# Weight units loaded seven ahead, up rows in dying buffers, and a new order of splits and fetches in a decoder block

## The chip, the cores and the metric

The kernel runs on one core of a Trainium2 chip. The metric is device time in microseconds for one execution; the median of three runs is given, and beside it the profile of one execution.

The engines are called PE (TensorE, matrix products), DVE (VectorE), ACT (ScalarE), POOL (GpSimd) and SP (SyncE). A core has 16 DMA engines. Plain transfers are issued here by SP and ACT, indirect ones (gathers by a table of row numbers) by GpSimd.

## The reference

One decoder block for 256 tokens of width 2048 in float32: attention and retention in parallel, an output projection, and then a retrieval layer over 16,384 experts, which is the part that the change touches:

```python
def peer(x, w_query, sub_keys, expert_down, expert_up):
    qry = (xt @ w_query).reshape(T, H, 2, PEER_HALF_DIM)
    s = jnp.einsum('thpd,phnd->thpn', qry, sub_keys)
    top_s, top_i = lax.top_k(s, K)                      # K = 16, H = 8
...
    best_s, best_pos = lax.top_k(cand_s.reshape(T, H, K * K), K)
    expert_idx = jnp.take_along_axis(cand_i.reshape(T, H, K * K), best_pos, axis=-1)
    gates = jax.nn.softmax(best_s, axis=-1)
...
        u = expert_down[ib]
        act = jax.nn.gelu(jnp.einsum('td,thkd->thk', xb, u), approximate=False)
        vv = expert_up[ib]
        return jnp.einsum('thk,thkd->td', gb * act, vv)
```

So each token picks 8 × 16 = 128 experts, takes the dot product of its row with each expert's down row, and sums the 128 up rows with the weights gate × gelu(dot product). The block's input is added, and a last RMSNorm follows.

## The kernel before

**Tokens and rows.** The 256 tokens are two blocks of 128, one token on each partition. "Row" below means one gather: for one of the 2 × 128 pairs of block and choice, each partition receives the expert row that its token chose. There are so 256 down rows, 256 up rows (128x2048, 1 MB each) and 256 scores (128x1).

**Up to 888 us** the projections, attention, retention, the output projection and the query projection run, all as matrix products whose float32 weights are cut in two on the way: ACT casts a half of a weight unit (128 x 4 x 512, 1 MB) to the reduced float32 type that PE takes fast (`whi`, line 109) and DVE subtracts that from the original (`wlo`, line 110). Each product of a chunk is then three matmuls: hi·hi, hi·lo, lo·hi. Units are loaded by SP into three buffers `raw`, and `next_unit` (line 126) has a unit loaded and split two ahead of its use.

**The gemm stage, to 1412 us.** The dot products of all tokens with all 16,384 down rows would be 256 x 16,384 numbers over 2048 columns. The kernel computes 11 of the 16 column chunks in this way, on PE, in 32 tiles of 512 experts: 8 chunks as split products (48 matmuls, two units) and 3 chunks unsplit in float32 (12 instructions, one unit, line 163). The result `a`, scaled by ACT (line 479), is written to `a_dram`. The last tile takes all 11 chunks unsplit (line 174). For the other 5 chunks (640 columns) only the chosen experts are wanted. When the indices `ix` of the top-k are ready (line 606), GpSimd gathers the 640 columns of each down row into a ring of eight buffers `v` (`fetch_u`, line 617), and DVE takes 256 dot products (`dot`, line 625), each with its sum in `sdot`. Each dot product issues the fetch eight later, and the last eight issue the first eight up rows in the same buffers (line 595).

**The last stage.** GpSimd fetches the score of each pair of token and expert from `a_dram` into `wsel` (line 652). For each group of eight choices DVE adds the dot products' part (line 694), ACT takes the gelu (line 695), DVE multiplies by the gates (line 696), and then DVE adds the eight up rows, each times its weight, to `ys` in PSUM (line 704). After row n the score n+14 and the up row n+8 are issued (lines 707 to 710), in one fixed line on GpSimd (`in_line`, line 658). `finish` does the last norm and writes the block's output.

**What sets the order.** Each engine runs its own instructions in order and waits by semaphores. Where the code sets no order, a scheduler that works on estimates places the instructions; DVE's background work of the gemm stage (top-k, then dot products) is drawn from a list by costs (`drain`).

## Time and profile before

| what | before |
|---|---|
| median of 3 runs | 2150.22 us (2147.36 to 2151.7) |
| profiled execution | 2149.12 us |
| its span | 2147.3 us |
| busy PE / DVE / ACT / POOL | 1391.4 / 1550.4 / 613.7 / 920.1 us |
| mean granted clock of PE, share of full speed | 0.828 |
| moved by DMA | 630.24 MB, 293 GB/s over the span |

The span is measured from the first to the last instruction on the device, and the profiled execution's time is 1.8 us more. All rows below come from that execution. Times are in us from the span's start, unless marked otherwise; "mean ns" is one instruction's mean duration, and a busy PE is not PE at its peak. In a row of a timeline, the first number is the start, the second how long the run of equal instructions took, `x6` how many they are, and the square brackets give the engine's idle time just before and what ended it ("issue": nothing that the profile shows).

### The profile page before, as it was taken

To read this page: it belongs to the slowest core of one execution; us is meant where nothing else is said; L and a number is where in the kernel's file an instruction comes from. 1 tells how busy PE (TensorE), PEld (TensorE's weight loads), DVE (VectorE), ACT (ScalarE), POOL (GpSimd) and SP (SyncE) were. 2 spreads that over 40 slices of the span, in tenths; PEclk is the share of its full clock that TensorE was granted. 3 is DMA by queue.
4 is the path that set the end of the run, shared out by engine and by line. 5 is a ranking of instruction groups with operands and counts; after the bars stand their busy time and mean duration, and the time that the engine had idled before them with its cause. 6 is when DMAs were issued, how large, how long until landed. Compare 5 with 4: busy or idle time off the path is not lost.

```text
span 2147.3 us, 18694 instructions
## 1 busy us (share of the span) xinstructions
PE 1391.4 (65%) x5848; PEld 1075.2 (50%) x5848; DVE 1550.4 (72%) x2026; ACT 613.7 (29%) x780; POOL 920.1 (43%) x805
## 2 busy tenths in 40 slices
PE   8999999999999999999999999930000000000000
PEld 6888888888888888766666666610000000000000
DVE  5676575545445567896778777739889888988888
ACT  6555444444444454433333333200000001000001
POOL 0101001000000010008888888847667677777774
PEclk9999999999999999999999999965555555555555
DMA  8544445655555564469999999959999999999997
GB/s 301 182 155 173 176 150 185 234 192 190 188 195 196 177 237 170 160 219 369 404 409 408 405 410 401 406 218 399 365 362 399 351 396 356 397 371 370 380 368 316
DMA packets 115604, 630.24 MB, mean 293 GB/s; under 512 B 22448, under 2 KB 23088, under 8 KB 55088
## 3 DMA queue, kind: packets, MB, share of 16 engines
q0 software_dynamic: 65536, 352.50, 42.1%
q1 hardware_dynamic: 38592, 253.77, 32.3%
q10 hardware_dynamic: 11376, 22.77, 2.8%
q8 instruction: 46, 0.75, 0.1%
q14 instruction: 54, 0.44, 0.1%
HBM read 610.10 MB, written 18.87 MB: 293 GB/s over the span
## 4 chain that ended last, share of the span: by engine, by line
PE 45%; issue 16%; DMA 15%; POOL 11%; DVE 8%; POOLq 4%; ACT 0%; ACTq 0%; DVEq 0%; SPq 0%
PE acc L141 13%; PE acc L142 13%; PE acc L140 12%; DMA v<-in_down_g_dram,ix 10%; POOL v L595 4%; POOL wsel L652 4%; DVE ys L704 4%; POOLq L595 3%; DMA v<-in_up_dram,ix 3%; POOL v L617 2%; DVE wlo L110 2%; POOLq L652 1%; PE acc L163 1%; DVE djunk L625 1%; DMA wsel<-a_dram,ix 1%
## 5 line engine op out<-in xcount | busy, mean ns | idle before, releaser
L110 DVE TENSOR_TENSOR wlo<-raw,whi 128x1024 fp32r<-128x1024 f32 (+1 forms) x422 | 522.0, 1239 | 331.7 <-ACT whi L109 330.7
L704 DVE SCALAR_TENSOR_TENSOR ys<-v,wsel,ys 128x2048 f32<-128x2048 f32 x252 | 593.5, 2355 | 63.3 <-DMA v<-in_up_dram,ix 41.9
L109 ACT CAST whi<-raw 128x1024 fp32r<-128x1024 f32 (+1 forms) x422 | 439.6, 1048 | 664.8 <-PE acc L142 369.6
L617 POOL DMA_INDIRECT v<-in_down_g_dram,ix x256 | 342.3, 1337 | 258.3 <-issue 226.0
L595 POOL DMA_INDIRECT v<-in_up_dram,ix x256 | 259.6, 1014 | 114.3 <-issue 94.4
L652 POOL DMA_INDIRECT wsel<-a_dram,ix x256 | 259.6, 1014 | 100.6 <-issue 77.7
L141 PE MATMUL acc<-wlo,xth 128*128 128x512 f32 x736 | 292.9, 398 | 0.5 <-DVE wlo L110 0.5
L142 PE MATMUL acc<-whi,xtl 128*128 128x512 f32 x736 | 288.9, 393 | 0.0
L625 DVE SCALAR_TENSOR_TENSOR djunk<-v,rs_r,hg 128x640 bf16<-128x640 f32 x256 | 218.9, 880 | 96.5 <-DMA v<-in_down_g_dram,ix 89.8
L140 PE MATMUL acc<-whi,xth 128*128 128x512 f32 x736 | 267.4, 395 | 8.9 <-ACT whi L109 8.9
L157 PE MATMUL acc<-wlo,hth 128*128 128x512 f32 x496 | 196.8, 397 | 9.5 <-DVE wlo L110 5.7
L158 PE MATMUL acc<-whi,htl 128*128 128x512 f32 x496 | 193.7, 391 | 0.0
L156 PE MATMUL acc<-whi,hth 128*128 128x512 f32 x496 | 186.0, 412 | 1.7 <-ACT whi L109 1.7
L695 ACT ACTIVATE wsel<-wsel 128x8 f32<-128x8 f32 x32 | 6.7, 208 | 626.8 <-DVE wsel L694 215.1
L163 PE MATMUL acc<-raw,htf 128*128 128x512 f32 x372 | 164.6, 592 | 0.0
L140 PEld LDWEIGHTS acc<-whi,xth 128*128 128x128 f32 x736 | 139.0, 189 | 38.2 <-ACT whi L109 9.3
L141 PEld LDWEIGHTS acc<-wlo,xth 128*128 128x128 f32 x736 | 139.5, 190 | 30.2 <-DVE wlo L110 1.2
L142 PEld LDWEIGHTS acc<-whi,xtl 128*128 128x128 f32 x736 | 139.5, 190 | 28.4 <-issue 0.2
L444 POOL TENSOR_TENSOR sg<-sg 128x512 f32<-128x512 f32 x8 | 14.1, 1790 | 291.8 <-DVE sg L443 291.8
L157 PEld LDWEIGHTS acc<-wlo,hth 128*128 128x128 f32 x496 | 93.1, 188 | 37.2 <-DVE wlo L110 11.9
L156 PEld LDWEIGHTS acc<-whi,hth 128*128 128x128 f32 x496 | 93.2, 188 | 31.7 <-issue 12.0
L163 PEld LDWEIGHTS acc<-raw,htf 128*128 128x128 f32 x372 | 70.5, 189 | 76.7 <-issue 74.2
(189 smaller groups left out, 1521.5 us busy)
## 6 DMA issues: line engine op xcount, KB each, us to landing
raw<-in_w_in_dram SPq DMA_DIRECT2D x91, 1024.0 KB
raw<-in_down_dram SPq DMA_DIRECT2D x64, 1024.0 KB
raw<-in_down_n_dram SPq DMA_DIRECT2D x32, 768.0 KB
raw<-in_w_rb_dram SPq DMA_DIRECT2D x16, 1024.0 KB
raw<-in_w_out_dram SPq DMA_DIRECT2D x16, 1024.0 KB
raw<-in_w_q_dram SPq DMA_DIRECT2D x16, 1024.0 KB
a_dram<-a ACTq DMA_DIRECT2D x64, 256.0 KB
raw<-in_w_ab_dram SPq DMA_DIRECT2D x8, 1024.0 KB
```

The source lines that it names most:

```text
L109: nc.scalar.copy(hi[:, k:k + step], src)
L110: nc.vector.tensor_sub(lo[:, k:k + step], src, hi[:, k:k + step].bitcast(F32))
L140: nc.tensor.matmul(ps[b], lhsT=xh, rhs=wh, start=(c == 0), stop=False)
L141: nc.tensor.matmul(ps[b], lhsT=xh, rhs=wl, start=False, stop=False)
L142: nc.tensor.matmul(ps[b], lhsT=xl, rhs=wh, start=False, stop=(c == last))
L156: nc.tensor.matmul(ps[b], lhsT=xh, rhs=wh, start=(c == 0), stop=False)
L157: nc.tensor.matmul(ps[b], lhsT=xh, rhs=wl, start=False, stop=False)
L163: nc.tensor.matmul(ps[b], lhsT=xf[:, CF + k, b * P:(b + 1) * P], rhs=nat[:, k], start=False, stop=(k == CN - 1))
L595: return nc.gpsimd.indirect_dma_start(v, None, up, IndirectOffsetOnAxis(ap=ix[:, 0, b, k:k + 1], axis=0), bounds_check=NE - 1)
L617: nc.gpsimd.indirect_dma_start(u[:, :GC], None, down_g, IndirectOffsetOnAxis(ap=ix[:, 0, b, k:k + 1], axis=0), bounds_check=NE - 1)
L652: return nc.gpsimd.indirect_dma_start(wsel[:, b, k:k + 1], None, a_flat[b], IndirectOffsetOnAxis(ap=ix[:, 1, b, k:k + 1], axis=0), bounds_ ...
L704: nc.vector.scalar_tensor_tensor((h[:, b] if last else ys)[:, cs], v[:, cs], w[:, kk:kk + 1], (h[:, b] if first else ys)[:, cs], op0=OP.mu ...
```

## The change

**Weight units.** In the gemm stage the units go through a ring of seven 1 MB buffers in place of three: two new ones, the three old ones, and two that held the second half of the split, transposed input, which the gemm stage doesn't read. A unit is loaded six ahead of the one in use. Split halves go to five buffers `whl` (hi and lo in one) in place of three and three.

**Splits.** The second half of each split unit from 16 units ahead of the gemm stage up to its tile 4 is subtracted on GpSimd, not DVE: 26 subtractions of 128x1024. In the gemm stage each subtraction of unit u is placed behind dot product number int(9.6 × (tile − 4)), by `paced`.

**Down rows.** They have their own twelve buffers of 128x640 in place of eight of 128x2048. The elementwise output of the dot product, which nobody reads, goes to PSUM as float32 and no longer to SBUF as bf16. The last norm's weights `fbc` are loaded when the indices are made.

**Up rows and scores.** Up rows go into fourteen buffers that the gemm stage has done with: the seven of the weight ring, the five of the halves, and two more. All are issued behind the last down row: six up rows, the scores 0 to 7, then one up row and one score in turn, and in the steady state the score n+14 and the up row n+14 behind row n.

```diff
+UR = 12
+R2 = 2
+CYC = R2 + 5
+WHL = 5
+EARLY = 6
+PACE = 9.6
+FIRST = 4
...
+    dots = []
+
+    def paced(u):
+        due = min(int(PACE * ((u - base) / 3 - FIRST)), len(dots)) - 1
+        return tc.issue_after(dots[due].ins) if u >= base and due >= 0 else nullcontext()
...
                 nc.scalar.copy(hi[:, k:k + step], src)
-                nc.vector.tensor_sub(lo[:, k:k + step], src, hi[:, k:k + step].bitcast(F32))
+                eng = nc.gpsimd if i and base - 16 <= u < base + 15 else nc.vector
+                with paced(u):
+                    eng.tensor_sub(lo[:, k:k + step], src, hi[:, k:k + step].bitcast(F32))
...
     def next_unit():
         u = state["used"]
         state["used"] += 1
+        if u >= base:
+            load_to(u + CYC - 1)
+        elif u >= base - 16:
+            load_to(base + min(R2 - 1, (u - base + 14) // 4))
+            if u >= base - 2:
+                load_to(u + 2)
         prefetch(u + 2)
...
+    first_row = 3 * NT
+    ring = [("s", i) for i in range(first_row, first_row + CYC - 3)] + [("w", i) for i in range(WHL)] + [("x", 0), ("x", 1)]
+    ring += [("s", i) for i in range(first_row + CYC - 3, first_row + CYC)]
+    RING = len(ring)
...
-        nc.vector.scalar_tensor_tensor(junk, u[:, :GC], rstd2[:, b:b + 1], hg[:, b], op0=OP.mult, op1=OP.mult,
-                                       accum_out=sdot[:, b, k:k + 1])
-        if n + VR < NB * P:
-            fetch_u(n + VR)
-        else:
-            fetch(n + VR - NB * P)
+        dots.append(nc.vector.scalar_tensor_tensor(vp["junk"][:, :GC], u, rstd2[:, b:b + 1], hg[:, b], op0=OP.mult, op1=OP.mult,
+                                       accum_out=sdot[:, b, k:k + 1]))
+        if n + UR < NB * P:
+            fetch_u(n + UR)
...
+    line = {"last": vp["last_u"]}
...
+    for n in range(EARLY):
+        in_line(fetch, n)
+    row = EARLY
     for n in range(LEAD):
         in_line(score, n)
+        if n >= GRP - 1:
+            in_line(fetch, row)
+            row += 1
+    for n in range(row, RING):
+        in_line(fetch, n)
...
                 if n + LEAD < total:
                     in_line(score, n + LEAD)
-                if n + VR < total:
-                    in_line(fetch, n + VR)
+                if n + RING < total:
+                    in_line(fetch, n + RING)
```

GpSimd from the last down rows to the scores (`v` and `u` are down rows or up rows by their source, `raw`, `v_w` and `v_x` the buffers of up rows, `wsel` the scores). Before:

```order
L617 DMA v<-in_down_g_dram,ix 128x640 x256
L595 DMA v<-in_up_dram,ix 128x2048 x8
L652 DMA wsel<-a_dram_5667,ix 128x1 x15
L595 DMA v<-in_up_dram,ix 128x2048
L652 DMA wsel<-a_dram_5667,ix 128x1
```

The same place on GpSimd in the changed kernel:

```order
L707 DMA u<-in_down_g_dram,ix 128x640 x256
L682 DMA raw_xh_10192<-in_up_dram,ix 128x2048
L682 DMA raw_xl_10196<-in_up_dram,ix 128x2048
L682 DMA raw_10200<-in_up_dram,ix 128x2048
L682 DMA raw_10204<-in_up_dram,ix 128x2048
L682 DMA v_w<-in_up_dram,ix 128x2048 x2
L742 DMA wsel<-a_dram_5406,ix 128x1 x8
L682 DMA v_w<-in_up_dram,ix 128x2048
L742 DMA wsel<-a_dram_5406,ix 128x1
L682 DMA v_w_10247<-in_up_dram,ix 128x2048
```

Six up rows stand ahead of the first score where eight stood, and after eight scores, not fifteen, rows and scores take turns.

GpSimd at the end of the program, before:

```order
L652 DMA wsel<-a_dram_5668,ix 128x1
L595 DMA v<-in_up_dram,ix 128x2048
L652 DMA wsel<-a_dram_5668,ix 128x1
L595 DMA v<-in_up_dram,ix 128x2048 x7
L771 UNCONDITIONAL_BRANCH
```

and in the changed kernel:

```order
L742 DMA wsel<-a_dram_5407,ix 128x1
L682 DMA raw_xl_12333<-in_up_dram,ix 128x2048
L742 DMA wsel<-a_dram_5407,ix 128x1
L682 DMA raw_12344<-in_up_dram,ix 128x2048
L742 DMA wsel<-a_dram_5407,ix 128x1
L682 DMA raw_12352<-in_up_dram,ix 128x2048
L860 UNCONDITIONAL_BRANCH
```

The last score had seven up rows behind it and now has one.

VectorE about the tiles 11 and 12 of the gemm stage (`wlo`, `whl`: splits; `djunk,sdot` and `ys,sdot`: dot products, `x4` four in a row). Before:

```order
L110 TENSOR_TENSOR wlo<-raw,whi 128x1024
L625 SCALAR_TENSOR_TENSOR djunk,sdot<-v,rs_r,hg 128x640
L110 TENSOR_TENSOR wlo<-raw,whi 128x1024
L625 SCALAR_TENSOR_TENSOR djunk,sdot<-v,rs_r,hg 128x640 x4
L110 TENSOR_TENSOR wlo<-raw,whi 128x1024
L625 SCALAR_TENSOR_TENSOR djunk,sdot<-v,rs_r,hg 128x640
```

and in the changed kernel:

```order
L714 SCALAR_TENSOR_TENSOR ys,sdot<-u,rs_r,hg 128x640 x9
L173 TENSOR_TENSOR whl_7611<-raw_xh_7428,whl_7611 128x1024
L173 TENSOR_TENSOR whl<-raw_xh_7428,whl 128x1024
L714 SCALAR_TENSOR_TENSOR ys,sdot<-u,rs_r,hg 128x640 x4
L173 TENSOR_TENSOR whl<-raw_xl_7469,whl 128x1024 x2
L714 SCALAR_TENSOR_TENSOR ys,sdot<-u,rs_r,hg 128x640 x9
```

Single splits stood between single and four dot products, ten of these to a tile; now both splits of a unit stand together, and twelve to thirteen dot products come to a tile here, 9.6 from tile 13 on.

## Rows read from the trace of the kernel before

**Rows 1.** Busy time in four stretches of the span. Columns: stretch (us), its length; then busy us and number of instructions of PE, PE's weight loads, DVE, ACT and POOL; PE's granted clock, share of the 16 DMA engines, GB/s.

```profile
888.00:972.00 84.00, 82.30 (x312) 57.60 (x311) 76.41 (x256) 30.33 (x35) 4.68 (x5) 1.00 0.62 210
972.00:1390.00 418.00, 408.50 (x1506) 281.42 (x1505) 324.75 (x605) 134.54 (x148) 339.44 (x254) 1.00 1.01 402
1390.00:1418.00 28.00, 22.04 (x52) 9.49 (x50) 2.59 (x6) 2.75 (x4) 6.93 (x7) 0.97 0.95 389
1418.00:2122.00 704.00, 0.00 (x0) 0.00 (x0) 602.43 (x329) 17.43 (x49) 510.50 (x504) 0.50 0.94 365
```

**Rows 2.** Groups of instructions between 972 and 1410 us, each shape apart: down-row fetches, dot products, splits. Behind the count: busy us, mean ns of one, idle time of the engine just before them and what ended it.

```profile
L617 POOL DMA_INDIRECT v<-in_down_g_dram,ix x252 | 338.1, 1342 | 78.3 <-issue 46.0 <-DVE wlo L110 15.2 <-DVE djunk L625 13.3
...
L625 DVE SCALAR_TENSOR_TENSOR djunk<-v,rs_r,hg 128x640 bf16<-128x640 f32 x256 | 218.9, 880 | 96.5 <-DMA v<-in_down_g_dram,ix 89.8 <-issue 6.6
...
L110 DVE TENSOR_TENSOR wlo<-raw,whi 128x1024 fp32r<-128x1024 f32 x99 | 120.7, 1221 | 1.9 <-ACT whi L109 1.5 <-issue 0.4
```

**Rows 3.** The down-row fetches of line 617 alone in two stretches: stretch, length, POOL's busy us and number; PE's clock, DMA share, GB/s.

```profile
966.00:1091.00 125.00, 101.57 (x77) 1.00 1.00 389
966.00:1387.00 421.00, 341.73 (x256) 1.00 1.01 401
```

**Rows 4.** Timeline of DVE in the gemm stage: two dot products.

```profile
1070.20 0.88 DVE L625 SCALAR_TENSOR_TENSOR djunk<-v,rs_r,hg 128x640 bf16<-128x640 f32 x1 [0.68 <-DMA v<-in_down_g_dram,ix]
...
1072.61 0.89 DVE L625 SCALAR_TENSOR_TENSOR djunk<-v,rs_r,hg 128x640 bf16<-128x640 f32 x1 [1.51 <-DMA v<-in_down_g_dram,ix]
```

**Rows 5.** Timeline of PE: the unsplit unit of the first tile, two neighbouring matmuls, the unsplit unit of the last tile but one (line 163), the last tile (line 174).

```profile
888.16 2.31 PE L163 MATMUL acc<-raw,htf 128*128 128x512 f32 x5
...
1367.66 0.39 PE L157 MATMUL acc<-wlo,hth 128*128 128x512 f32 x1
1367.88 0.39 PE L158 MATMUL acc<-whi,htl 128*128 128x512 f32 x1
...
1387.85 5.31 PE L163 MATMUL acc<-raw,htf 128*128 128x512 f32 x12
1392.99 19.05 PE L174 MATMUL acc<-raw,htf 128*128 128x512 f32 x44
```

**Rows 6.** Timeline of POOL in the last stage: an up row and a score.

```profile
1460.22 1.01 POOL L595 DMA_INDIRECT v<-in_up_dram,ix  x1 [0.30 <-issue]
1461.53 1.01 POOL L652 DMA_INDIRECT wsel<-a_dram,ix  x1 [0.30 <-issue]
```

**Rows 7.** Timelines of POOL and DVE in the last stage: a late fetch (the up row 41), and a run of six row steps, the first of them of row 34.

```profile
1528.95 1.01 POOL L595 DMA_INDIRECT v<-in_up_dram,ix  x1 [2.51 <-issue]
...
1515.59 14.31 DVE L704 SCALAR_TENSOR_TENSOR ys<-v,wsel,ys 128x2048 f32<-128x2048 f32 x6
```

**Rows 8.** Two of the costliest groups of the whole span, columns as in rows 2: the row steps, and the casts ahead of the splits.

```profile
L704 DVE SCALAR_TENSOR_TENSOR ys<-v,wsel,ys 128x2048 f32<-128x2048 f32 x252 | 593.5, 2355 | 63.3 <-DMA v<-in_up_dram,ix 41.9
L109 ACT CAST whi<-raw 128x1024 fp32r<-128x1024 f32 (+1 forms) x422 | 439.6, 1048 | 664.8 <-PE acc L142 369.6
```

**Rows 9.** Timelines of DVE and POOL: the first group's step on DVE, and the end (the last score, the last up row, the last group's step on DVE).

```profile
1430.02 0.17 DVE L694 TENSOR_TENSOR wsel<-wsel,sdot 128x8 f32<-128x8 f32 x1 [35.25 <-DMA wsel<-a_dram,ix]
...
2111.50 1.01 POOL L652 DMA_INDIRECT wsel<-a_dram,ix  x1 [0.30 <-issue]
...
2120.69 1.00 POOL L595 DMA_INDIRECT v<-in_up_dram,ix  x1 [0.30 <-issue]
...
2116.18 0.17 DVE L694 TENSOR_TENSOR wsel<-wsel,sdot 128x8 f32<-128x8 f32 x1 [0.64 <-DMA wsel<-a_dram,ix]
```

**Rows 10.** Groups on POOL, columns as in rows 2: two additions of 128x1024 that it does once, ahead of the gemm stage.

```profile
L471 POOL TENSOR_TENSOR htf<-hth,htl 128x1024 f32<-128x1024 f32 x2 | 5.8, 2910 | 0.0
```

**Rows 11.** Timelines of POOL and DVE about 780 us: three additions on POOL, a split on DVE beside them, and a split behind them.

```profile
779.42 7.59 POOL L471 TENSOR_TENSOR htf<-hth,htl 128x768 f32<-128x768 f32 x3 [86.94 <-PE acc L142]
...
780.47 1.89 DVE L110 TENSOR_TENSOR wlo<-raw,whi 128x1024 fp32r<-128x1024 f32 x1 [0.30 <-ACT whi L109]
...
786.96 1.21 DVE L110 TENSOR_TENSOR wlo<-raw,whi 128x1024 fp32r<-128x1024 f32 x1
```

**Rows 12.** Timelines of POOL and DVE: the first down-row fetch and the first dot product.

```profile
966.10 1.19 POOL L617 DMA_INDIRECT v<-in_down_g_dram,ix  x1 [179.08 <-issue]
...
972.30 0.88 DVE L625 SCALAR_TENSOR_TENSOR djunk<-v,rs_r,hg 128x640 bf16<-128x640 f32 x1 [3.24 <-DMA v<-in_down_g_dram,ix]
```

**Rows 13.** Between the down rows and the scores: timeline of POOL (the first and the eighth up row, the first score), of ACT (the last tile's second result), and, from the chain of waits, that result's write to `a_dram` and the transfer of a score.

```profile
1387.90 1.01 POOL L595 DMA_INDIRECT v<-in_up_dram,ix  x1 [0.30 <-DMA v<-in_down_g_dram,ix]
...
1397.75 1.00 POOL L595 DMA_INDIRECT v<-in_up_dram,ix  x1 [0.30 <-issue]
...
1418.31 1.01 POOL L652 DMA_INDIRECT wsel<-a_dram,ix  x1 [19.56 <-DMA a_dram<-a]
...
1409.50 0.69 ACT L479 ACTIVATE a<-acc,rs_r 128x512 f32<-128x512 f32 x1 [15.33 <-PE acc L174]
...
1410.22 7.26 DMA a_dram<-a
...
1427.52 2.38 DMA wsel<-a_dram,ix
```

**Rows 14.** What POOL waited for between 1418 and 2122 us, of the up-row fetches: us in total, times, longest.

```profile
POOL v L595 <- issue: 92.9, 223, 2.5
...
POOL v L595 <- DVE ys L704: 15.5, 21, 2.5
```

More of the change, by code (lines that the diff above doesn't have):

```diff
@@ L1 @@
 from collections import deque
-from contextlib import ExitStack
+from contextlib import ExitStack, nullcontext
 import numpy as np
@@ L36, with __init__, __getitem__ @@
 DOT = 0.85
-VR = 8
+UR = 12
[5 more added lines that the diff above has]
+FIRST = 4
 GRP = 8
 LEAD = 14
+class Halves:
+    def __init__(self, pool, name, tag):
+        self.parts = [pool.tile([P, NC // 2, T], F32R, name=f"{name}{i}", tag=f"{tag}{i}") for i in range(2)]
+    def __getitem__(self, key):
+        c = key[1]
+        i = (c.start if isinstance(c, slice) else c) // (NC // 2)
+        if isinstance(c, slice):
+            c = slice(c.start - 8 * i, c.stop - 8 * i)
+        else:
+            c -= 8 * i
+        return self.parts[i][(key[0], c) + tuple(key[2:])]
 @with_exitstack
@@ L88, in hybrid_block, with slot, half, load_unit @@
     ready = {}
-    def emit_unit(u):
-        if u in native:
-            nat = stream.tile([P, 4, 512], F32, name="raw", bufs=3)
-            nc.sync.dma_start(nat[:, :units[u].shape[1]], units[u])
-            ready[u] = nat
-            return
-        raw = stream.tile([P, 4, 512], F32, name="raw", bufs=3)
+    base = len(units) - 3 * NT
+    raws = {}
+    sp = {"half": 0}
+    def slot(i):
+        c = i % CYC
+        if c < R2:
+            return sp["raw2"].tile([P, 4, 512], F32, name="raw2", bufs=R2)
+        if c < R2 + 3:
+            return stream.tile([P, 4, 512], F32, name="raw", bufs=3)
+        t = ("xh1", "xl1")[c - R2 - 3]
+        return keep.tile([P, 4, 512], F32, name="raw_" + t, tag=t)
+    def half(u):
+        n = 0
+        if u >= base:
+            n = sp["half"] % WHL
+            sp["half"] += 1
+        if n < 3:
+            return stream.tile([P, 2, 2, 512], F32R, name="whl", bufs=3)
+        return sp["raw2"].tile([P, 2, 2, 512], F32R, name="whl2", bufs=WHL - 3)
+    def load_unit(u):
+        if u < base:
+            raw = stream.tile([P, 4, 512], F32, name="raw", bufs=3)
+        else:
+            raw = slot(u - base)
+        raws[u] = raw
         if u == 0:
@@ L100, in emit_unit, with load_to @@
         else:
-            nc.sync.dma_start(raw, units[u])
+            nc.sync.dma_start(raw[:, :units[u].shape[1]], units[u])
+    def load_to(u):
+        while state["loaded"] < len(units) and state["loaded"] <= u:
+            with tc.high_priority(100000):
+                load_unit(state["loaded"])
+            state["loaded"] += 1
+    dots = []
+    def paced(u):
+        due = min(int(PACE * ((u - base) / 3 - FIRST)), len(dots)) - 1
+        return tc.issue_after(dots[due].ins) if u >= base and due >= 0 else nullcontext()
+    def emit_unit(u):
+        if u < base:
+            load_unit(u)
+        raw = raws.pop(u)
+        if u in native:
+            ready[u] = raw
+            return
         hs = []
         for i in range(2):
-            hi = stream.tile([P, 2, 512], F32R, name="whi", bufs=3)
-            lo = stream.tile([P, 2, 512], F32R, name="wlo", bufs=3)
+            both = half(u)
+            hi, lo = both[:, 0], both[:, 1]
             step = 1 if u == 0 else 2
@@ L121, in prefetch @@
             state["emitted"] += 1
+    state["loaded"] = base
     def next_unit():
@@ L466, in hybrid_block @@
     peer = pool("peer")
+    sp["raw2"] = pool("raw2")
     h_ops = pair_ops(hth, htl)
@@ L606, in indices @@
         nc.vector.tensor_copy(ix, ef)
-        vp["pool"] = pool("v")
+        vp["pool"] = pool("u")
         vp["ps"] = pool("ysum", space=PSUM)
-        for n in range(VR):
+        vp["junk"] = vp["ps"].tile([P, D], F32, name="ys")
+        vp["fbc"] = vp["pool"].tile([P, D], F32, name="fbc")
+        nc.scalar.dma_start(vp["fbc"], bass.AP(tensor=fin.tensor, offset=fin.offset, ap=[[0, P], [1, D]]))
+        for n in range(UR):
             fetch_u(n)
@@ L643, in hybrid_block, with in_line @@
     drain(1e9)
+    line = {"last": vp["last_u"]}
+    def in_line(fn, n):
+        with tc.issue_after(line["last"].ins):
+            line["last"] = fn(n)
     wsel = peer.tile([P, NB, P], F32, name="wsel")
```

40 lines of the change are left out of this document (20 added, 20 removed).

## The prediction

> **What bounds the kernel now.** I read the stretches of the span first (busy time per engine, clock, DMA share), then grouped lines and engine timelines. The reader is to see four stretches [rows 1]. From 888 to 972 us TensorE is busy 82.3 of 84 us. From 972 to 1390 nothing has slack in sum: TensorE 408.5 of 418, the DMA engines at a share of 1.01 with 402 GB/s, GpSimd 339. From 1390 to 1418 only the last matmul tile and its result run. From 1418 to 2122 VectorE is busy 602 of 704 and GpSimd 510.5, the DMA engines at 0.94.
>
> In the second stretch the sequence is GpSimd, then DMA, then VectorE, then TensorE. A fetch of a down row takes 1342 ns with 0.31 us idle ahead of it (78.3/252) [rows 2]; 256 of them fill 966 to 1387 without idling, 1.65 us a row [rows 3]. VectorE then waits 0.68 to 1.51 us for a row's landing before a dot product [rows 4] and, in one in-order queue, the splits stand behind the dot products. TensorE's tile could go faster: two neighbouring matmuls start 0.22 to 0.23 us apart, so 48 of the split kind plus 5.14 us for the unsplit unit (1392.99 less 1387.85) make about 16.0 us a tile, while 30 tiles take (1387.85 − 888.16)/30 = 16.66 [rows 5].
>
> In the last stretch GpSimd issues 504 fetches back to back [rows 1]. Two neighbours start 1.31 us apart [rows 6], so 504 need 662 us of the 703.4 between 1418.31 and 2121.7; the other 41 us are gaps in stretches, such as the 2.51 us ahead of the fetch at 1528.95 [rows 7]. VectorE's row is 2355 ns [rows 8], its group of eight 18.8 us and about one more for the weights' gelu, under 16 × 1.314 = 21.0 us of GpSimd. So this stretch is GpSimd's, and a group's first step on VectorE waits for the group's last score [rows 9].
>
> **The change, part by part.** The sum is made against the profiled execution: 2149.12 us, of which 2147.3 are span and 1.8 lie around it; the median of the three runs is 2150.22, 1.1 above it.
>
> *Splits to GpSimd (26 of 128x1024: 16 in the query projection, 10 in tiles 0 to 4).* On GpSimd an add of that shape takes 2.91 us against 1.22 on VectorE [rows 10, 2]. Two halves are 24 matmuls, 24 × 0.22 to 0.23 = 5.4 us [rows 5]; a cast of 1.05 [rows 8] and a split of 2.91 come to 3.96, so TensorE should not see it. Nine of these stand ahead of the indices on VectorE: 9 × 1.2 = 11 us less there. Against it, VectorE's two-input work slows beside GpSimd's: the split at 780.47 took 1.89 us under an add of GpSimd, the later one 1.21 [rows 11], 0.67 each, some six times, 4 us. So the first row fetch moves from 966.1 [rows 12] by −11 + 4 = −7 to 959, with 957 and 961 as ends.
>
> The Trainium skill's page "SBUF — State Buffer", section "Who interferes with whom", has the rule behind the sentence on 780.47: VectorE's instruction with two SBUF inputs contends with a GpSimd instruction that reads SBUF. The trace agrees (1.89 against 1.21), and by it this part of the change is paid for twice. Were the rule without effect here, the 4 us would fall away and the first fetch come at 955.
>
> *Splits behind numbered dot products.* Before, splits follow 62 dot products at tile 12 and 142 at tile 20, ten a tile. Now 76 stand ahead of tile 12's, then 9.6 a tile. At the unchanged rate row 76 is issued 123.5 us after the first (77 fetches between 966 and 1091 [rows 3]), lands 6.2 later (966.10 to 972.30 [rows 12]), then 0.9 for the dot product, 1.2 for the split, 19 tiles of 16.03 and the last of 19.05: 455 us from the first fetch to TensorE's end. The later gates come to between 451 and 455. Before, it is 1412.04 − 966.10 = 446. The new gates thus eat what the earlier start gives: 959 + 453 = 1412, where it was: 0 us (957 + 451 to 961 + 455: −4 to +4).
>
> *Units loaded seven ahead.* Four more units of 1 MB can arrive before the stretch whose DMA share is 1.01; at 402 GB/s that is 10 us of its transfer time. It counts only if GpSimd's 1.65 us a row falls too; I take nothing, with 0 to −10 as ends, since VectorE's two-input work beside the fetches stays.
>
> *Dot products' throw-away output to PSUM, 640 float columns for bf16.* Its duration there isn't in this trace; the row product into PSUM, 2355 ns for 2048 columns, and today's dot product, 880 for 640, lie on one line (1.05 ns a column plus 0.21 us) [rows 2, 8], so 0 (−0.05 to +0.1 us each, beside 96.5 us of waits).
>
> *Up-row and score fetches behind the down rows.* Before, eight up rows are issued between 1387.90 and 1397.75, and then GpSimd stands 19.56 us, since the next is a score, which needs the last tile's result: written from 1410.22 on in 7.26 us, while 8 MB of rows are still landing [rows 13]. Now six rows are issued, two fewer in that write's way; a small transfer alone takes 2.38 us, so the write can lose between 0 and 4.9 us. I take half, −2.4.
>
> *Fourteen rows deep.* Before, the row n+8 and score n+14 follow row n; now both n+14. So the number of fetches behind the first score is 506 for 504, at the same pitch, and the ring's depth gives nothing to an engine that is the bound. But the last score moves. Before, it is fetch 496 after the first (2111.50); the last group starts when it lands (2116.18) and the span ends some 31 us on, while the seven up rows behind it are issued in that time, until 2120.69 [rows 9]. Now it is number 504, with all rows ahead of it but one: 8 × 1.314 = 10.5 us later for the last group and the end. Ends: 0 if the pitch falls by as much, 14 if GpSimd is in a slow stretch (8 × 1.75).
>
> *Rest.* The last norm's weights, now loaded when the indices are made (1 MB, 2.5 us at 402 GB/s, beside down rows), and four score buffers for six: nothing, hidden by TensorE's own tiles, 0 to +2.
>
> Sum: 2149.12 + 0 − 2.4 + 10.5 = 2157.2; I say 2157, 0.3 to 0.4% above both times of before.
>
> **Rivals.**
>
> *A. The ring hides GpSimd's gaps.* The waits of that stretch put 15.5 us on a row buffer's release by VectorE, and 92.9 on nothing shown [rows 14]. If the 41 us come from buffers, fourteen of them take them away: 2157 − 41 = 2116. Against it: the fetch at 1528.95 came 2.51 us late though the row that had its buffer before (33) was done when the six rows from 1515.59 on began [rows 7], 13 us before.
>
> *B. The gemm stage falls to TensorE's floor.* Early units, GpSimd's splits off VectorE and 12 rows in flight let the rows land ahead of the gates. Then 30 tiles save 30 × (16.66 − 16.03) = 19 us, of which I count 17, since the first tiles ahead of the dot products are at the floor already: 2157 − 17 = 2140. For it: TensorE is the largest busy sum. Against it: a DMA share of 1.01 [rows 1], from which only the 10 us of early units go; and the gates at 12 to 13 dot products a tile in tiles 7 to 12.
>
> *C. GpSimd's splits hold TensorE up: slower still.* They decide once a cast and a split take longer than two halves, 5.4 us. 2.91 is for an add with little beside it. Slowed as 1.21 was to 1.89, it makes 4.5, 5.6 with the cast, 0.2 over; at twice 2.91 it makes 6.9, 1.5 over. At 0.8, between them, 26 splits cost 21 us: 2178. Against it: the other half of each unit stays with VectorE, and three halves are buffered.
>
> *D. The six early rows or the last score don't do what the order says*, because VectorE catches up in the last groups: the tail's +10.5 is gone: 2147. For it: VectorE's own 602 us are 100 under the stretch [rows 1]. Against it: the last score's place is fixed by the order.
>
> **How the numbers follow.** Forecast 0.45, of which 0.07 is D, with a range of its own of 2143 to 2167 (gates −4 to +4, write 0 to −4.9, tail 0 to 14, the rest 0 to 2). A 0.15, B 0.20, C 0.20. What differs by less than 0.2%, 2145.9 to 2154.5, can't be told from no change. Faster: A 0.15, B 0.18, forecast 0.03: 0.36. Within: forecast 0.17, B 0.02, C 0.03: 0.22. Slower: forecast 0.25, C 0.17: 0.42. The range that holds 8 in 10 leaves out most of A below and the worst of C above: 2118 to 2176.
>
> **What the profile after would show.** First down-row fetch at 957–961; matmul tiles of 16.0 us from tile 12 on and TensorE's end at 1408–1415; GpSimd idle for some 20 to 25 us ahead of the first score; fetches of the last stretch at 1.31 us with the same slow stretches; each group of eight starting with its last score, and the last score 8 fetches nearer the end. Wrong: a pitch of down rows well under 1.65 us (B), no gaps over 0.3 us among GpSimd's 506 fetches (A), or TensorE waiting for a split by GpSimd (C).

## The result and the profile after

The changed kernel takes 2182.64 us (2180.69 to 2186.48, six runs) against 2150.05 for the kernel before: ratio 1.0149, 95% interval [1.0137, 1.0160], 32.6 us slower. The forecast was slower, but 2157; the time lies above the range of 2118 to 2176.

The profiled executions have spans of 2147.3 and 2181.9 us, 34.6 apart. Two places hold all of it. The first score is issued at 1442.5 for 1418.3, 24.2 later; and from there to the end of the span it is 739.4 for 729.0, 10.4 longer.

Busy time by stretch after, in the stretches of [rows 1] (PE, PE's weight loads, DVE, ACT, POOL; clock, DMA share, GB/s):

```profile
888.00:972.00 84.00, 84.00 (x328) 59.75 (x327) 77.18 (x257) 31.70 (x38) 24.30 (x11) 1.00 0.59 214
972.00:1390.00 418.00, 388.27 (x1404) 266.01 (x1403) 326.68 (x573) 129.25 (x140) 343.66 (x242) 0.98 0.99 382
1390.00:1418.00 28.00, 26.92 (x99) 18.02 (x98) 23.24 (x39) 5.92 (x7) 19.69 (x15) 1.00 0.99 372
1418.00:2122.00 704.00, 25.29 (x69) 12.67 (x67) 573.06 (x313) 17.20 (x49) 497.61 (x489) 0.52 0.94 364
```

TensorE, 408.5 us busy between 972 and 1390 before, is busy 388.3 there now, and its 1404 matmuls are about 100 fewer; the DMA engines move 382 GB/s for 402. The stage has become slower in all its parts at once, which points to a wait that they share.

That wait stands in two views. What PE waited for between 1000 and 1120 us:

```profile
PE acc L228 <- DVE whl L173: 10.6, 4, 7.6
PE acc L228 <- issue: 4.1, 1, 4.1
PE acc L227 <- ACT whl L170: 2.6, 1, 2.6
```

and what DVE waited for there:

```profile
DVE ys L714 <- DMA u<-in_down_g_dram,ix: 28.6, 17, 5.6
```

PE waits for splits, DVE for down rows, with the splits queued behind. One of these in the timelines (DVE, then PE):

```profile
1087.39 0.89 DVE L714 SCALAR_TENSOR_TENSOR ys<-u,rs_r,hg 128x640 f32<-128x640 f32 x1 [5.60 <-DMA u<-in_down_g_dram,ix]
1090.13 0.89 DVE L714 SCALAR_TENSOR_TENSOR ys<-u,rs_r,hg 128x640 f32<-128x640 f32 x1 [1.79 <-DMA u<-in_down_g_dram,ix]
1090.94 2.36 DVE L173 TENSOR_TENSOR whl<-raw_xl,whl 128x1024 fp32r<-128x1024 f32 x2
...
1092.22 0.80 PE L228 MATMUL acc<-whl,hth 128*128 128x512 f32 x1 [7.62 <-DVE whl L173]
```

The splits at 1090.94 stand behind 67 dot products. The rows for the last of these are not there, so TensorE stands 7.62 us. The unsplit units of tiles 7 to 13 start 22.9, 18.4, 21.8, 26.9, 17.2 and 17.8 us apart, where most undisturbed tiles take 16.1.

The groups on POOL and DVE that answer to [rows 2] (fetches of the whole span; dot products between 966 and 1420):

```profile
L707 POOL DMA_INDIRECT u<-in_down_g_dram,ix x256 | 363.1, 1418 | 97.7 <-issue 31.4 <-DVE ys L714 28.0 <-DVE ix L693 19.1
...
L714 DVE SCALAR_TENSOR_TENSOR ys<-u,rs_r,hg 128x640 f32<-128x640 f32 x256 | 229.1, 895 | 100.7 <-DMA u<-in_down_g_dram,ix 94.6 <-issue 1.3 <-DVE ys L714 0.2
```

A fetch takes 1418 ns for 1337 over the whole span; the dot product itself 895 for 880. The first fetch, and the end of the stage (POOL; then ACT's first result of the last tile, for one block of tokens):

```profile
966.50 1.92 POOL L707 DMA_INDIRECT u<-in_down_g_dram,ix  x1 [19.09 <-DVE ix L693]
...
1407.02 1.19 POOL L707 DMA_INDIRECT u<-in_down_g_dram,ix  x1 [0.30 <-issue]
...
1428.11 1.00 POOL L682 DMA_INDIRECT raw<-in_up_dram,ix  x1 [11.79 <-PE acc L234]
...
1442.51 1.02 POOL L742 DMA_INDIRECT wsel<-a_dram,ix  x1 [10.78 <-issue]
...
1433.88 0.69 ACT L551 ACTIVATE a<-acc,rs_r 128x512 f32<-128x512 f32 x1 [5.03 <-PE acc L245]
```

The first down row comes at 966.50, not earlier than before [rows 12]; the last 20.4 us later than before. The result at 1433.88 is what the first score waits for; its counterpart before, at 1409.50, is labelled the last tile's second result in [rows 13] but is the first of its two. Even the fourth early up row waits 11.79 us, because its buffer is a weight buffer that TensorE still reads.

The kernel before itself took 2147 to 2153 us beside experiments 1 to 3 and 2108 to 2120 beside all later ones (three executions of the study, of 2463 and twice 4345 us, are left out), so times are compared as ratios to the runs of before beside them; run `b_again` shows where the difference lies.

### The profile page after: what moved, and what is told of

Same layout as the page of the kernel before. It is cut to its first block, busy times and chain, and to the rows that moved or that the text cites. A ratio compares the mean times of both kernels' runs of the same rounds, so it can differ in the third digit from the quotient of the medians.

```text
span 2181.9 us, 18706 instructions
## 1 busy us (share of the span) xinstructions
PE 1399.3 (64%) x5848; PEld 1078.8 (49%) x5848; DVE 1560.5 (72%) x2000; ACT 612.1 (28%) x778; POOL 1011.9 (46%) x831
## 4 chain that ended last, share of the span: by engine, by line
PE 44%; issue 19%; DMA 12%; DVE 11%; POOL 9%; POOLq 4%; ACT 0%; DVEq 0%; SPq 0%; ACTq 0%
PE acc L212 12%; PE acc L213 12%; PE acc L211 12%; DMA u<-in_down_g_dram,ix 8%; DVE ys L793 6%; POOL wsel L742 4%; POOLq L682 3%; DVE whl L173 2%; PE acc L234 2%; DMA wsel<-a_dram,ix 2%; DVE ys L714 2%; PE acc L228 2%; PE acc L227 1%; PE acc L229 1%; POOLq L742 1%
## 5 line engine op out<-in xcount | busy, mean ns | idle before, releaser
L173 DVE TENSOR_TENSOR whl<-raw,whl 128x1024 fp32r<-128x1024 f32 (+1 forms) x365 | 453.1, 1250 | 331.5 <-ACT whl L170 331.2
L170 ACT CAST whl<-raw 128x1024 fp32r<-128x1024 f32 (+1 forms) x388 | 405.8, 1048 | 538.7 <-PE acc L213 355.3
L707 POOL DMA_INDIRECT u<-in_down_g_dram,ix x256 | 363.1, 1418 | 97.7 <-issue 31.4
L714 DVE SCALAR_TENSOR_TENSOR ys<-u,rs_r,hg 128x640 f32<-128x640 f32 x256 | 229.1, 895 | 100.7 <-DMA u<-in_down_g_dram,ix 94.6
L212 PE MATMUL acc<-whl,xth 128*128 128x512 f32 x736 | 292.4, 398 | 0.5 <-DVE whl L173 0.5
L213 PE MATMUL acc<-whl,xtl 128*128 128x512 f32 x736 | 288.5, 393 | 0.0
L211 PE MATMUL acc<-whl,xth 128*128 128x512 f32 x736 | 266.7, 394 | 8.3 <-ACT whl L170 8.3
L228 PE MATMUL acc<-whl,hth 128*128 128x512 f32 x496 | 199.7, 403 | 25.3 <-DVE whl L173 16.0
L793 DVE SCALAR_TENSOR_TENSOR ys<-raw,wsel,ys 128x2048 f32<-128x2048 f32 x90 | 212.0, 2356 | 3.2
L793 DVE SCALAR_TENSOR_TENSOR ys<-v_w,wsel,ys 128x2048 f32<-128x2048 f32 x90 | 212.0, 2356 | 3.2
L227 PE MATMUL acc<-whl,hth 128*128 128x512 f32 x496 | 185.1, 405 | 5.5 <-ACT whl L170 4.2
L211 PEld LDWEIGHTS acc<-whl,xth 128*128 128x128 f32 x736 | 138.6, 189 | 37.7 <-ACT whl L170 8.7
L212 PEld LDWEIGHTS acc<-whl,xth 128*128 128x128 f32 x736 | 139.2, 189 | 30.0 <-DVE whl L173 1.2
L682 POOL DMA_INDIRECT raw<-in_up_dram,ix x92 | 92.9, 1010 | 59.5 <-issue 34.8
```

Source lines behind the costliest of these rows:

```text
L170: nc.scalar.copy(hi[:, k:k + step], src)
L173: eng.tensor_sub(lo[:, k:k + step], src, hi[:, k:k + step].bitcast(F32))
L211: nc.tensor.matmul(ps[b], lhsT=xh, rhs=wh, start=(c == 0), stop=False)
L212: nc.tensor.matmul(ps[b], lhsT=xh, rhs=wl, start=False, stop=False)
L213: nc.tensor.matmul(ps[b], lhsT=xl, rhs=wh, start=False, stop=(c == last))
L227: nc.tensor.matmul(ps[b], lhsT=xh, rhs=wh, start=(c == 0), stop=False)
```

## The experiments

**1. Where does the dot product write?**

```diff
-        dots.append(nc.vector.scalar_tensor_tensor(vp["junk"][:, :GC], u, ...
+        junk = peer.tile([P, GC], BF16, name="djunk", bufs=1)
+        dots.append(nc.vector.scalar_tensor_tensor(junk, u, ...
```

> The changed kernel with the dot products' throw-away output back in SBUF as bf16 (one buffer). Theory P (an output in PSUM makes VectorE's dot product hold up GpSimd's fetch longer): the mean down-row fetch falls from 1418 to about 1337 ns, 256 of them end about 20 us earlier, TensorE's end comes 15 to 22 us earlier, time 2161 to 2168. Rival D (the fetch is slower because twelve down rows and seven weight units load the DMA engines): mean fetch stays within 20 ns of 1418, time 2180 to 2186.

Measured: 2183.73 us, ratio 1.0142 [1.0123, 1.0161]; mean fetch 1403 ns. The last down row came 5.0 us earlier, the first score at 1442.3. Theory P fails here: the fetch is 15 ns shorter, not 81, and two profiles of the changed kernel's own gemm stage differ by as much (1418 here, 1437 in experiment 3). But this run is not the output of before: that went to two SBUF buffers in turn, this goes to one.

The output moved to PSUM, alone, in the kernel before (there too one buffer takes the place of two):

```diff
-        nc.vector.scalar_tensor_tensor(junk, u[:, :GC], ...
+        nc.vector.scalar_tensor_tensor(vp["junk"][:, :GC], u[:, :GC], ...
```

> The kernel before with the dot products' output in PSUM as float32, nothing else. Theory P: mean down-row fetch from 1337 to about 1418 ns, the last down row about 20 us later, time 2163 to 2172. Rival D: fetch and time as before, 2147 to 2153.

Measured: 2162.48 us, ratio 1.0059 [1.0042, 1.0075]; between the two theories. The group of fetches (columns as in [rows 2]):

```profile
L618 POOL DMA_INDIRECT v<-in_down_g_dram,ix x256 | 352.9, 1378 | 257.6 <-issue 212.9 <-DVE ys L625 28.7 <-DVE wlo L110 12.2
```

1378 for 1337: half of what P wants, and more than three profiles of the stage of before differ (1323, 1336, 1337). So the output's new place, one tile in PSUM, does lengthen GpSimd's fetches, but the change has another cause for the rest. VectorE's own instruction hardly changes (893 for 880), yet the next one starts later. Two dot products back to back before, in the changed kernel, and in `a_sbuf`:

```profile
1379.83 0.88 DVE L625 SCALAR_TENSOR_TENSOR djunk<-v,rs_r,hg 128x640 bf16<-128x640 f32 x1
1380.64 0.88 DVE L625 SCALAR_TENSOR_TENSOR djunk<-v,rs_r,hg 128x640 bf16<-128x640 f32 x1
...
1099.14 0.89 DVE L714 SCALAR_TENSOR_TENSOR ys<-u,rs_r,hg 128x640 f32<-128x640 f32 x1
1100.12 0.89 DVE L714 SCALAR_TENSOR_TENSOR ys<-u,rs_r,hg 128x640 f32<-128x640 f32 x1
...
1096.11 0.89 DVE L714 SCALAR_TENSOR_TENSOR djunk<-u,rs_r,hg 128x640 bf16<-128x640 f32 x1
1097.04 0.89 DVE L714 SCALAR_TENSOR_TENSOR djunk<-u,rs_r,hg 128x640 bf16<-128x640 f32 x1
```

In the median they start 0.81 us apart with two SBUF buffers, 0.99 with one in PSUM (0.99 in `b_psum` too) and 0.93 with one in SBUF. Two thirds of the 0.18 us thus come with the single buffer. What PSUM alone does to the fetches, and what two SBUF buffers would give back in the changed kernel, no run shows.

**2. The gates.**

```diff
-FIRST = 4
+FIRST = 6
```

> The changed kernel with FIRST 6 for 4: each split placed behind 19 dot products fewer. Theory G (the gates of tiles 7 to 12 cost TensorE 25 us that it never gets back): those tiles fall from 17 to 27 us to about 16 to 17.5, the first result of the last tile (1433.9) comes 18 to 25 us earlier, time 2158 to 2166. Rival W (the dot products only move to the end: down rows still end at 1407 and all up rows wait for them): first score 10 us earlier at most, time 2172 to 2180.

Measured: 2167.69 us, ratio 1.0081 [1.0064, 1.0097]. PE between 1002 and 1117 us, this run first, then the changed kernel (columns as in [rows 1]):

```profile
1002.00:1117.00 115.00, 113.75 (x424) 79.12 (x423) 92.02 (x159) 38.58 (x42) 93.56 (x68) 1.00 1.01 402
```

```profile
1002.00:1117.00 115.00, 96.71 (x337) 66.37 (x336) 86.44 (x154) 30.79 (x33) 94.46 (x68) 0.93 0.95 358
```

TensorE is busy 17 us more of the same 115, the DMA engines are full again, and the granted clock, 0.93 of full speed in the mean where TensorE stood between matmuls, is 1.00, the 2.4 GHz level. Tiles 7 to 12 take 16.1 to 17.1 us. The first score comes at 1418.7, 23.8 earlier, where the kernel before has it. GpSimd issues its 68 fetches in either case. So theory G holds for the gemm stage. The time fell by 15 us only; in this profile first score to end is 744.1 for 739.4, and experiment 8 shows that gaps on GpSimd account for 4.3 of the 4.7.

**3. The tail.**

```diff
-LEAD = 14
+LEAD = 21
...
-        if n >= GRP - 1:
+        if n >= GRP - 1 and row < RING:
```

> The changed kernel with scores 21 ahead for 14, the ring of up rows left at 14: the last score has eight up rows behind it, as before. Theory T (the last group waits for the last score, which stands behind all up rows but one): first score to end falls from 739 to 729 to 731, time 2172 to 2176. Rival R (the last group is then late by its up rows, which come no earlier): 739 and 2180 to 2186.

Measured: 2176.5 us, ratio 1.0113 [1.0096, 1.0130]; first score to end 734.0 for 739.4 in the profile. Of the 10.4 us 5.4 come back: the last group no longer waits for its score (VectorE's step on it follows the row before without a wait), and now its rows set the end, 38.6 us behind the last score for 35.0. This profile is of an execution of 2186.45 us; its gemm stage is the same program as the changed kernel's, and yet its first score came at 1450.7 for 1442.5. Differences of a few us between single profiles are therefore no evidence by themselves.

**4. The splits on GpSimd.**

```diff
-                eng = nc.gpsimd if i and base - 16 <= u < base + 15 else nc.vector
+                eng = nc.vector
```

> The changed kernel with all splits on VectorE. Theory S (the splits on GpSimd, first of all the three about 787 us that stand behind its additions, cost TensorE 6 us ahead of the gemm stage): the first unsplit unit of the gemm stage moves from 894 back to 887 to 889; the first down-row fetch goes the other way, since VectorE has 9 splits more ahead of the indices: 968 to 976. The gates hang on that fetch, so the time gets worse or stays: 2182 to 2190. Rival Q (the GpSimd splits buy nothing, the first fetch is late because TensorE is): first fetch 958 to 965, time 2174 to 2180.

Measured: ratio 1.0124 [1.0104, 1.0144] for 1.0149 [1.0137, 1.0160]; the intervals overlap. PE's first unsplit unit, in this run and in the changed kernel (each row ends with the window shown):

```profile
886.78 3.59 PE L234 MATMUL acc<-raw,htf 128*128 128x512 f32 x8
```

```profile
894.21 2.74 PE L234 MATMUL acc<-raw,htf 128*128 128x512 f32 x6
```

TensorE enters the stage 7.4 us earlier, as S says; but the first fetch comes at 961.00, not later: there Q is right. The place of the loss in the changed kernel (POOL, then PE):

```profile
775.90 2.41 POOL L173 TENSOR_TENSOR whl<-raw,whl 128x1024 fp32r<-128x1024 f32 x1 [85.31 <-ACT whl L170]
778.27 7.58 POOL L543 TENSOR_TENSOR htf<-hth,htl 128x768 f32<-128x768 f32 x3
785.80 2.37 POOL L173 TENSOR_TENSOR whl<-raw,whl 128x1024 fp32r<-128x1024 f32 x1
791.51 8.69 POOL L173 TENSOR_TENSOR whl<-raw,whl 128x1024 fp32r<-128x1024 f32 x3 [3.34 <-ACT whl L170]
...
788.23 0.50 PE L212 MATMUL acc<-whl,hth 128*128 128x512 f32 x1 [1.26 <-POOL whl L173]
797.34 0.50 PE L212 MATMUL acc<-whl,hth 128*128 128x512 f32 x1 [2.30 <-POOL whl L173]
```

TensorE stands three times here, 4.3 us in all. The first wait, 1.26 us, is for a split that stands behind three additions of 7.58 us on the same queue. The longest, 2.30 us, is for one of three splits in a row, which began when ACT's cast was done and took 2.9 us each in the mean; the third, 0.77 us, is for a split on VectorE. Behind them the granted clock is 0.81 of full speed from 796 to 800 and 0.76 from 800 to 804, where `a_nogps` has 1.00 throughout; that is another 1.7 us, by an estimate (4 × 0.19 + 4 × 0.24), so some 6 of the 7.4 us are accounted for. Most splits take 2.4 us on GpSimd, less than the 2.91 that I had taken; four of the 26 take 3.0 to 4.4.

**5. Why a fetch lasts longer.** In the changed kernel's timelines of the gemm stage (DVE, then POOL):

```profile
1138.29 2.36 DVE L173 TENSOR_TENSOR whl<-raw,whl 128x1024 fp32r<-128x1024 f32 x2
...
1136.94 1.01 POOL L707 DMA_INDIRECT u<-in_down_g_dram,ix  x1 [0.30 <-DVE ys L714]
1138.26 1.01 POOL L707 DMA_INDIRECT u<-in_down_g_dram,ix  x1 [0.30 <-issue]
1139.58 1.96 POOL L707 DMA_INDIRECT u<-in_down_g_dram,ix  x1 [0.30 <-DMA u<-in_down_g_dram,ix]
```

The fetch that starts just ahead of the two splits takes 1.01 us; the one that starts in the second of them ends 0.9 us after it. One that starts in the first of a pair (DVE, then POOL):

```profile
1043.16 2.36 DVE L173 TENSOR_TENSOR whl<-raw,whl 128x1024 fp32r<-128x1024 f32 x2
...
1043.44 1.83 POOL L707 DMA_INDIRECT u<-in_down_g_dram,ix  x1 [0.31 <-DVE ys L714]
```

It ends at 1045.27, 0.9 us after the first split (1.22 us long) and 0.25 ahead of the end of the second. Sorted by what VectorE did at their start, the 256 fetches (number, mean us) are:

```
                      before       changed      FIRST 6, halves apart
VectorE idle          71  1.01     59  1.01     66  1.01
in a dot product     133  1.40    148  1.43    141  1.42
in a split            52  1.63     49  1.88     49  1.76
all                  256  1.337   256  1.418    256  1.380
```

In the changed kernel the 49 that start in splits last 0.92 us plus 0.97 times what was left of that one split (correlation 0.98). No fetch is held for both splits of a pair: 21 start in the first one, last 1.78 us and end 0.9 us after it, inside the second; 25 start in the second, with 1.09 us of it left, and last 1.98 (three start in single splits). The changed order puts both splits of a unit together (as the order shown with the change has it), and a fetch then more often starts near the beginning of a split: on average about 1.0 us is left, 0.8 before.

```diff
-        due = min(int(PACE * ((u - base) / 3 - FIRST)), len(dots)) - 1
+        due = min(int(PACE * ((u - base) / 3 - FIRST)) + 4 * i, len(dots)) - 1
```

> The changed kernel with FIRST 6, and the second half's split placed four dot products behind the first half's, so that no two splits stand together. Theory B (a fetch that is issued while VectorE runs a split or a dot product lasts until that is over, and two splits in a row hold it for both): the fetches that start under a split fall from 1.88 to about 1.63 us in the mean, the mean fetch from 1416 to 1360 to 1380 ns, the last down row 9 to 14 us earlier than with FIRST 6 alone (1408.6); the time then follows the end of the last tile: 2158 to 2168. Rival D (the fetch is longer because of the rows and units in flight): mean fetch within 15 ns of 1416.

Measured: ratio 1.0041 [1.0023, 1.0060] for 1.0081 with FIRST 6 alone; mean fetch 1380 for 1416 ns, the last down row 11.2 us earlier, at 1397.4. The fetches that start in splits fall to 1.76, half of the way to 1.63; the mean and the last row come out as theory B has them, but not by its reason, since a pair holds no fetch for both. So the pairs are a part of the other cause that experiment 1 left open: 36 ns against `a_first6`, 21 against a second profile of its gemm stage (1401 ns, `a_f6_lead30`). With the output in SBUF as well, the three runs of experiments 7 and 9 have 1361, 1386 and 1381 ns, still some 45 above before; that rest is not explained, and the single output buffer and the more rows in flight are untested for it. Nor does the earlier last row reach the first score: it comes at 1418.9 for 1418.7. In `a_first6` GpSimd issued it 0.3 us behind the sixth up row; here the six go out from 1398.7 on, and GpSimd stands 12.3 us for the write of the last tile's result, which is issued at 1406.0 beside them. Where the gain in time lies is not shown.

**6. More scores ahead, alone and with FIRST 6.**

```diff
-LEAD = 14
+LEAD = 30
```

> The kernel before with scores 30 ahead for 14. Theory T (the end hangs on where the last score stands in GpSimd's line): the last score stands 16 pairs earlier, the last group waits for its up rows instead, first score to end falls from 729 to 719 to 724, time 2140 to 2146. Rival R (the last rows were as late as the last score, or the later up rows at the stage's start cost as much): 727 to 730, time 2148 to 2152.

Measured: ratio 1.0116 [1.0086, 1.0147], slower, against both theories' sign and size. The last stage in three stretches (columns as in [rows 1]):

```profile
1416.00:1466.00 50.00, 0.00 (x0) 0.00 (x0) 21.81 (x16) 1.91 (x4) 38.73 (x38) 0.50 0.14 47
1466.00:2050.00 584.00, 0.00 (x0) 0.00 (x0) 527.14 (x291) 15.31 (x44) 448.80 (x444) 0.50 1.01 400
2050.00:2098.00 48.00, 0.00 (x0) 0.00 (x0) 44.60 (x22) 0.21 (x1) 23.47 (x24) 0.50 1.01 416
```

While GpSimd issues thirty scores, no up row can follow: the DMA engines are at 0.14 for 50 us (0.55 in the kernel before from 1418 to 1468), and then at 1.01 to the end, also when the scores are all out. What the rows lost there cannot be caught up. I had counted GpSimd's fetches only, and the DMA engines are the next bound right behind it.

> The changed kernel with FIRST 6 and scores 30 ahead. If gates and tail are all that made the change slower, the two gains add up: first score about 1419, first score to end 719 to 724 for 739, time 2146 to 2152. If the pitch of the down rows is a bound of its own, the first score stays at 1419 or later and the time at 2155 to 2165.

Measured: ratio 1.0074 [1.0046, 1.0101]: no better than FIRST 6 alone, for the same reason (the DMA engines are at 0.57 from 1418 to 1470 and near 1.0 after that); first score at 1415.0, and from there to the end 708.9 us.

**7. All mended together, and the tail once more.** Five edits: FIRST 6, halves four dot products apart, no split on GpSimd, dot products' output in SBUF, scores 21 ahead; then the same with 14.

> The changed kernel with five edits: FIRST 6, halves of a unit split four dot products apart, all splits on VectorE, the dot products' output in SBUF as bf16, scores 21 ahead. If the four costs found so far are separate, TensorE enters the gemm stage at 887 to 888, down rows are fetched at 1.65 us as before, the first score comes at 1408 to 1414 and the end as long behind it as in the kernel before: 4 to 12 us faster than before, ratio 0.994 to 0.998. If they share one cause, so that mending one has mended the others, ratio 1.002 to 1.006 as with FIRST 6 and the halves apart.

> The same with scores 14 ahead. Theory T (the tail is the last score's place): first score to the last group's start longer by 8 fetches of 1.31 us, 10 us slower than with 21, ratio 0.999 to 1.003. Rival R (where GpSimd's fetches keep up with the rows, the rows set the end): the same time as with 21 within 3 us.

Measured: ratio 0.9976 [0.9965, 0.9986] with 21, which beats the kernel before as well as the changed one, and 1.0005 [0.9993, 1.0017] with 14. First score to end: 696.3 with 21, 704.3 with 14. With 14 the last group's step waits for its score (first row), with 21 it doesn't (second):

```profile
2082.77 0.17 DVE L783 TENSOR_TENSOR wsel<-wsel,sdot 128x8 f32<-128x8 f32 x1 [2.39 <-DMA wsel<-a_dram,ix]
```

```profile
2075.71 0.16 DVE L783 TENSOR_TENSOR wsel<-wsel,sdot 128x8 f32<-128x8 f32 x1
```

So the last score's place is worth 8.0 us between these two profiles and 6 between the two ratios. The gains found one by one (1.0149 less 0.0068 for the gates, 0.0040 for the halves, 0.0036 for the tail, 0.0025 for GpSimd's splits, 0.0007 for the output) add up to 0.9973. Each gain has an interval of its own, and the sum is good to about 0.005 (an estimate from these intervals), so that it comes within 0.0003 is in part luck; that the costs do not share one cause is shown by the 0.9976 itself, which lies below the 1.002 to 1.006 of the second case.

**8. The kernel before once more, for its profile.**

> The kernel before once more, for a profile on the chip of these runs: it tells which stretches differ from chip to chip. If it is 2110 to 2117 us, the time from the first score to the end is about 692 for 729, without the slow stretches of GpSimd; if it is about 2150, as in the profile that the prediction was made from.

Measured: 2109.33 us; first score at 1414.5, and 693.1 us from there to the end for 729.0. GpSimd's waits of that stage, to be read beside [rows 14]:

```profile
POOL wsel L652 <- issue: 70.1, 230, 0.3
POOL v L595 <- issue: 62.1, 204, 0.3
```

The gaps ahead of up-row fetches for which nothing is shown (92.9 us, up to 2.5 each) are 62.1 here, none over 0.3. Same program, same buffers: the slow stretches of GpSimd go with the execution, not with the ring of rows. No run tells what causes them.

They can be taken out of the tail. From the first score to the end, what GpSimd stood between its fetches, and the rest (us):

```
                                            stage    stood    rest
before, b_psum                           729.0-729.3  192.9   536.1-536.4
b_again                                     693.1     155.0   538.1
changed, a_sbuf, a_first6                739.4-744.1  192.4-196.7  547.0-549.4
a_nogps, a_f6_apart, a_best14            702.3-704.3  154.0-157.0  547.1-548.3
a_lead21, a_best21, a_b21_gps            696.3-734.0  155.1-191.8  541.1-542.4
```

So the changed order of the last stage costs 9 to 13 us in either kind of execution, and scores 21 ahead give back some 5 or 6 of them. The last 3 to 6 stay: with 21 the end lies 38 to 40 us behind the last score, 36 in the kernel before.

**9. GpSimd's splits in the version that won.**

> The version that beat both kernels (five edits, ratio 0.9976) with its splits on GpSimd again. Theory S (GpSimd's splits queue behind its three additions of 7.6 us, TensorE waits for them about 787 us, and all that follows is late): the first unsplit unit of the gemm stage at 893 to 895 for 888.3, first down-row fetch 3 to 6 us later than 963.5, the whole 4 to 8 us slower, ratio 0.9995 to 1.0015. Rival Q (what TensorE loses there is given back by the earlier indices or hidden behind the fetches): ratio 0.996 to 0.999.

Measured: ratio 0.9996 [0.9981, 1.0011] for 0.9976 [0.9965, 0.9986]. TensorE enters the stage at 894.0 for 888.3 and the first fetch comes at 966.3 for 963.5, as S says; but the first score comes at 1411.5 for 1411.1. The ratios lean to S (0.0020, 4 us) but their intervals overlap, and the score's place speaks for Q. What these splits cost once the gates are loose stays open; neither pair shows a gain from them.

## Why the prediction was wrong

The direction and the tail were right; the gemm stage was not. By its own steps:

- *Splits to GpSimd.* "TensorE should not see it" failed: it enters the gemm stage 6.0 us later (894.2 for 888.2). I had priced a split and a cast against two halves, and not what stands ahead of a split on its queue (1.26 us of waiting), splits that follow one another at 2.9 us each (2.30), or the lower granted clock behind these waits (0.76 to 0.81). The first down row was to come at 959 and came at 966.5. From TensorE's entry to the first fetch 5.6 us were gained (72.3 for 77.9), but the two pairs of runs with and without these splits put only 2 to 3 of them down to the splits (74.2 to 72.3 in experiment 4, 75.2 to 72.3 in 9), for the 7 of the forecast; the later entry took the gain back. Rival C had the right place and sign and, in part, the right reason, but 21 us for what took 6 from TensorE.
- *Splits behind numbered dot products.* This is the step that failed: 0 us in the sum, and the last tile's first result is 24.4 us late (1433.88 for 1409.50). I worked out the gate at tile 12 at the unchanged rate of rows and let 19 tiles follow at the floor. By that formula tile 12 can start 131.8 us after the first fetch (123.5 + 6.2 + 0.9 + 1.2), at 1098.3 here; TensorE began it at 1104.1, 5.8 later, having stood for the splits of the tiles before it: twelve to thirteen dot products come to each of these, 21 to 22 us at the measured pitch of 1.727 us a row. Tile 30 began at 1408.5 (the first matmuls of the two, PE):

```profile
1104.08 0.50 PE L227 MATMUL acc<-whl,hth 128*128 128x512 f32 x1
...
1408.52 0.50 PE L228 MATMUL acc<-whl,hth 128*128 128x512 f32 x1 [1.08 <-issue]
```

  So tiles 12 to 29 took 16.9 us each, not 16.03. Every later tile waits for 9.6 more rows, and at 1.727 us a row, not 1.65, that alone is 16.6. Over 18 tiles that makes 16 us. With the late first row (7.5) and the 5.8 it is 29; about 5 of them come back at the end, where part of the last tile ran early, and 24 are left. FIRST 6 has the same pitch of rows (mean fetch 1416 ns) and brings the first score 23.8 us earlier, so the late rows cost this much only through the gates. The numbers of the gates were in the order; my error was to take a row rate measured under another order for a constant, where a gate's slack was a few us. The sum also followed TensorE's end (1412.04), while the first score waits for the first of the last tile's two results.
- *The dot products' output to PSUM.* Costed at zero on VectorE, from −0.05 to +0.1 us each. The instruction itself is nearly so (895 for 880 ns), but the next dot product starts 0.18 us later, 0.12 of it with one buffer in place of two. On GpSimd the fetch is 41 ns longer, alone in the kernel before, and the kernel 0.59% slower. The sum had no term for either; in the changed kernel the output in one SBUF buffer gave 0.0007, nothing clear of the intervals.
- *Halves split together.* Not in the sum at all, though the order showed it: 36 or 21 ns a fetch by the two profiles to compare with, and 0.0040 in the ratio.
- *Units loaded six ahead of the one in use* (the prediction calls it seven). Taken as nothing; no run tries it alone. The DMA engines reach 402 GB/s again with FIRST 6, so no cost is seen.
- *Fewer early up rows ahead of the scores.* −2.4 forecast; from the last tile's first result to the first score it is 8.6 us for 8.8: nothing.
- *Fourteen rows deep, and the tail.* +10.5 forecast, 10.4 measured. The reason holds too: from the first to the last score it is 704.4 us for 693.2, and from there to the end 35.0 for 35.8. The term stands. Moving the last score forward gives back 5 to 8 us of it and not all, since then the rows set the end.
- *Rivals.* A is refuted: with fourteen buffers the stage is longer, not 41 us shorter, and without slow stretches the kernel before has some 5 of the 41 left with its eight buffers (667.4 us for the 662 of 504 fetches). B was not what happened, but FIRST 6 comes near its floor (16.5 us a tile). D did not happen.

The Trainium skill's rule in "SBUF — State Buffer", section "Who interferes with whom", was cited for VectorE's loss under GpSimd's additions (1.89 for 1.21 us). The rule is about a GpSimd instruction that reads SBUF. The fetches, which take their indices `ix` from there, fit it in the other direction: 1.01 us with VectorE idle, 1.63 or 1.88 under its splits; that the reading of `ix` is what is held, no run shows. The same section reports that `tensor_tensor`, which a split is, did not stall a DMA in its probe. Here it does, and the measurement decides. This direction matters more for the gemm stage, and I had counted the first only.

## What to carry to other kernels

A gate written as "behind instruction number k" is only as good as the rate of what it counts; leave it slack of several rows, or the fast engine stands and nothing gives the time back. Where one engine's instructions hold up another's, the other waits for the rest of the one instruction in which it starts, and not for a whole run of them (1.78 us in the first of two splits, 1.98 in the second, 1.01 beside an idle VectorE); so look at when it starts, and not at the mean. Before a term is set to zero because an instruction is as long as before, look at when the next one starts. And before more fetches of one kind are put ahead, look at which resource idles meanwhile: the second bound may be right behind the first.

## What was not expected of the hardware

- An indirect fetch issued inside VectorE's split ends about 0.9 us after that one split is over, whatever was left of it and also where a second split follows at once; one issued just ahead takes 1.01 us (experiment 5).
- Dot products of 0.88 to 0.89 us start 0.81 us apart with the output in two SBUF buffers in turn, 0.93 with one SBUF buffer and 0.99 with one in PSUM. With the last in place of the first, the fetches beside them take 1378 ns for 1337 in the mean; which of the two differences does it is not shown (experiment 1).
- In some executions GpSimd has stretches with gaps of up to 2.5 us between fetches, and the stage from the first score to the end is 36 us longer; in others, of the same program, none over 0.3.
